# Three of eight tiles with seven products in the second feed-forward matrix, one bank moved last, and a split end for the first feed-forward block

## The chip, the cores and the metric

One core of a Trainium2 chip runs the whole program: TensorE (PE; PEld is its weight load), VectorE (DVE), ScalarE (ACT), GpSimd (POOL) and SyncE (SP), which issues the weight transfers. The metric is the device time in microseconds of one execution. The median of three runs of the kernel before is 2309.98 us (2309.74 to 2311.31).

## The reference, cut to what matters

Two layers of attention and feed-forward on 256 tokens of width 2048, all in float32. The change lies in the two feed-forward blocks (hidden width 8192) and in what follows the first of them, the norm of the dilated attention:

```
def sq_relu_mlp(h, w1, w2):
    return jnp.square(jax.nn.relu(h @ w1)) @ w2
...
        g, w1, w2 = ffns[i]
        x = x + sq_relu_mlp(rms_norm(x, g), w1, w2)
    return rms_norm(x, final_norm)
```

## The kernel before

**Products.** Every float32 operand of a large matrix product is split into an upper and a lower part (`hi`, `lo`), and each product of 128x128 by 128x512 is made of three matmuls (`three`, L193: upper by upper, upper by lower, lower by upper), which add into one of eight PSUM banks.

**Tiles.** A feed-forward block runs over four groups `g` of 2048 hidden columns. Each group makes two products with the first matrix and two with the second (`cp` 0 and 1, 1024 output columns each). Such a product (`gemm_pair`) is eight steps, one for each 256 rows of the contraction; a step is called a tile here and has the number of its rows (`pair`, 0 to 7). A standard tile (kind `s`) makes eight products for the four output quadrants, 24 matmuls. A seven-product tile (kind `x`) is one level of the Strassen-Winograd scheme: sums of weight quadrants against sums of the left operand's, seven products, 21 matmuls. `FF_PAIRS = (3, 5)`: two of the eight tiles of each product have seven products. Their seven sums gather in banks called "1" to "7", and "2", "3", "4" and "S" are also the four quadrants of the standard tiles. After the last seven-product tile `begin` combines "1", "6", "7" and "5" into an SBUF tile `C`; after the last tile `end` adds "2", "4", "S" and "3" to it.

**Order of the work.** The program is written out by hand: the last loop goes over `steps`, and in step i each of four quarters emits its matmuls, then its tasks (transposes), the functions in `after`, and the preparation `prep(i + 2, n)` of the tile two steps later; at the end of a step come `evac`, the last quarter's preparation, the load of step i + 5, and `post`. Each engine works through its own instructions in this order. Preparing a standard tile is two casts on ACT (`wh`, L190) and two subtractions on DVE (`wl`, L191). Preparing a seven-product tile (`prep_x`) is on DVE three additions into `sums` (L136), a `wl` of 128x1024, the subtraction `ls` of 128x2048 (L133) after ACT's cast `hs` (L176), and a `wl` of 128x512.

**Hidden values.** After a product with the first matrix, ACT squares the positive part of `C`, TensorE transposes it in the second and third tile of the next product (L694), into the four banks in `ps.spare` (the coming product's "1", "6", "7" and "5", in this order), and `post` of `hidden` splits the result into `hT`. For a seven-product tile of the second matrix `post` copies the transposed pair out (`h`) and makes its sums on DVE (`sums_and_parts`: `c`, `h`, `hT`, `hs`); for the others DVE makes one subtraction `hT` from the bank.

**After the second matrix** `residual` adds `C` to x in two additions of 128x1024 (x<-x,C). In the last group the squares for the next norm and the transposes of x follow (`next_norm`, `next_done`). In the second block, the last product's two last tiles are done column half by column half (`split_end`), so that half of x is complete one tile early.

Of the kernel before, what the change touches and what calls it, by code (L numbers as in the profile page):

```python
# [47 lines left out]
def tile_encoder(ctx: ExitStack, tc: tile.TileContext, ins, out):  # L48
# [217 lines left out]
    def sum_banks():  # L266

        if ps.order is None:
            l = ps.pair
            a, b = (l + 1) % 3, (l + 2) % 3  # L270
            ps.order = [2 * a, 2 * a + 1, 2 * b, 2 * b + 1, 6, 7, 2 * l, 2 * l + 1]
        order, ps.order = ps.order, ps.order[4:] + ps.order[:4]
        ps.spare = order[4:]
        return {q: order[n] for n, q in enumerate(("2", "4", "S", "3", "1", "6", "7", "5"))}

    STD = {(0, 0): "2", (0, 1): "3", (1, 0): "4", (1, 1): "S"}

    def gemm_pair(w, cp, A, sums_of, order, finish, split_end=False):
# [13 lines left out]
        def product(bank, a, b, last):  # L292
            if not q:
# [4 lines left out]
        X = (("1", "A11", 2), ("2", "A12", 3), ("6", "S2", 6), ("7", "S3", 4), ("5", "S1", 5), ("4", "A22", 7),  # L298
             ("3", "S4", 1))

        for n, (kind, pair) in enumerate(order):
# [7 lines left out]
            else:  # L309
                def quarter(s, m, pair=pair, n=n):  # L310
                    tb, c = ((0, 0), (1, 0), (1, 1), (0, 1))[m]
# [33 lines left out]

        def end(m):
            C = q["C"]
            if m == 0:
                add(nc.vector, C[:, 0, :], C[:, 0, :], q["2"])
            elif m == 1:  # L350
                subtract(nc.vector, C[:, 2, :], q["4"], C[:, 2, :])
            elif m == 2:
                add(nc.vector, C[:, 3, :], C[:, 3, :], q["S"])
            else:
                add(nc.vector, C[:, 1, :], C[:, 1, :], q["3"])
# [306 lines left out]

    FF_PAIRS = (3, 5)
    FF_ORDER = [("x" if k in FF_PAIRS else "s", k) for k in range(8)]
    FF_LAST = [FF_ORDER[k] for k in (0, 1, 3, 2, 5, 4, 6, 7)]

# [5 lines left out]
    def ffn(norm, w1, w2, next_norm, next_done):  # L672
        for g in range(4):
            hT, sums = [None] * 4, {}

            def hidden(made, q, cp, hT=hT, sums=sums):
# [7 lines left out]
                for m, (tb, n) in enumerate(((0, 0), (1, 0), (1, 1), (0, 1))):  # L684
                    at_after(i, m, lambda tb=tb, n=n: squared_relu(tb, n))
                for r in range(4):
# [10 lines left out]
                    def post(r=r, held=held):  # L697
# [3 lines left out]
                        if pair in FF_PAIRS:  # L701
                            raw = scratch([P, 2, T], "h")
                            nc.scalar.copy(raw, held["t"])
                            sums[pair] = part.pool.tile([P, 2, 3, P], F32R, name="hs", tag="hsum", bufs=len(FF_PAIRS))
# [7 lines left out]
            for cp in range(2):  # L712
                gemm_pair(w1, 2 * g + cp, norm.xT, norm.sums, FF_ORDER, lambda made, q, cp=cp: hidden(made, q, cp))

            w2g = w2[4 * g:4 * (g + 1)]
            last = g == 3

            def residual(made, q, cp):
                if last and next_norm() in fin and cp == 1:
                    def early():  # L720
                        add(nc.vector, x[:, 0, D // 2:], x[:, 0, D // 2:], both(q, 0))
                        subtract(nc.vector, x[:, 1, D // 2:D - 512], x[:, 1, D // 2:D - 512], q["C"][:, 2, :])
                        add(nc.vector, x[:, 1, D - 512:], x[:, 1, D - 512:], q["C"][:, 3, :])
                    made[-3].evac.append(early)
                    for tb in range(2):
                        made[-2].evac.append(lambda tb=tb: add(
# [387 lines left out]
```

## Time and profile before

| | |
|---|---|
| median of 3 runs | 2309.98 us (2309.74 to 2311.31) |
| the profiled execution's own time | 2308.4 us |
| its span, first to last instruction | 2306.6 us |
| busy: PE, PEld, DVE, ACT, POOL | 2273.0, 1898.0, 1758.8, 1217.7, 0.7 us |
| mean granted TensorE clock | 0.998 |

The span lies 1.8 us below the execution's own time, and that time 1.6 us below the median of the runs. A row of a timeline gives the start, the time taken, the engine, the line, the operation with output and inputs, and in brackets the idle time before it with the instruction that ended it. Matmuls and VectorE instructions overlap their successors a little: the distance between two starts is what one costs in a full queue.

### The profile page before, as it was taken

To read this page: it belongs to the slowest core of one execution; us is meant where nothing else is said; L and a number is where in the kernel's file an instruction comes from. 1 tells how busy PE (TensorE), PEld (TensorE's weight loads), DVE (VectorE), ACT (ScalarE), POOL (GpSimd) and SP (SyncE) were. 2 spreads that over 40 slices of the span, in tenths; PEclk is the share of its full clock that TensorE was granted. 3 is DMA by queue.
4 is the path that set the end of the run, shared out by engine and by line. 5 is a ranking of instruction groups with operands and counts; after the bars stand their busy time and mean duration, and the time that the engine had idled before them with its cause. 6 is when DMAs were issued, how large, how long until landed. Compare 5 with 4: busy or idle time off the path is not lost.

```text
span 2306.6 us, 28352 instructions
## 1 busy us (share of the span) xinstructions
PE 2273.0 (99%) x10988; PEld 1898.0 (82%) x10988; DVE 1758.8 (76%) x2082; ACT 1217.7 (53%) x1526; POOL 0.7 (0%) x6
## 2 busy tenths in 40 slices
PE   9999999999999999999999999999999999999998
PEld 7888888888888888887788888888888888888886
DVE  6666766788788788788877667757888788788787
ACT  6444545564564564565444544456554654554554
POOL 0000000000000000000000000000000000000000
PEclk9999999999999999999999999999999999999999
DMA  7555655656656656655554555555666566566563
GB/s 250 173 175 174 193 185 167 191 181 210 186 182 206 194 177 208 200 167 180 178 198 167 184 171 181 175 172 161 184 209 187 183 205 196 182 201 201 182 219 128
DMA packets 110727, 430.33 MB, mean 187 GB/s; under 512 B 23872, under 2 KB 24448, under 8 KB 92160
## 3 DMA queue, kind: packets, MB, share of 16 engines
q1 hardware_dynamic: 109920, 426.82, 57.4%
q8 instruction: 86, 1.41, 0.2%
q10 hardware_dynamic: 672, 1.70, 0.2%
q14 instruction: 49, 0.40, 0.0%
HBM read 426.38 MB, written 2.10 MB: 186 GB/s over the span
## 4 chain that ended last, share of the span: by engine, by line
PE 87%; DVE 5%; ACT 5%; issue 2%; DMA 1%; SPq 0%; ACTq 0%; DVEq 0%
PE banks L195 22%; PE banks L196 22%; PE banks L197 22%; PE banks L220 13%; PE banks L222 6%; ACT wh L190 2%; DVE wl L191 1%; DVE sums L136 1%; DVE ls L133 1%; ACT C L681 1%; ACT hs L176 1%; PE banks L694 1%; PE banks L384 1%; ACT C L682 0%; DMA bias<-in_rpb_dram 0%
## 5 line engine op out<-in xcount | busy, mean ns | idle before, releaser
L191 DVE TENSOR_TENSOR wl<-w,wh 128x1024 fp32r<-128x1024 f32 (+1 forms) x802 | 931.5, 1176 | 389.5 <-ACT wh L190 385.7
L190 ACT CAST wh<-w 128x1024 fp32r<-128x1024 f32 (+1 forms) x802 | 804.6, 1014 | 691.6 <-PE banks L197 478.4
L220 PE MATMUL banks<-xT,wh 128*128 128x512 f32 x1280 | 455.6, 399 | 0.5 <-ACT wh L190 0.4
L195 PE MATMUL banks<-wh,xT 128*128 128x512 f32 x1152 | 453.7, 394 | 0.0
L197 PE MATMUL banks<-wh,xT 128*128 128x512 f32 x1152 | 449.3, 390 | 0.0
L196 PE MATMUL banks<-wl,xT 128*128 128x512 f32 x1152 | 448.6, 389 | 0.6 <-DVE wl L191 0.6
L222 PE MATMUL banks<-xT,wl 128*128 128x256 f32 x1280 | 358.5, 280 | 2.3 <-DVE wl L191 2.3
L195 PE MATMUL banks<-wh,hT 128*128 128x512 f32 x832 | 327.2, 393 | 0.0
L197 PE MATMUL banks<-wh,hT 128*128 128x512 f32 x832 | 324.4, 390 | 0.0
L196 PE MATMUL banks<-wl,hT 128*128 128x512 f32 x832 | 323.8, 389 | 0.0
L220 PEld LDWEIGHTS banks<-xT,wh 128*128 128x128 f32 x1280 | 241.6, 189 | 55.6 <-ACT wh L190 1.5
L197 PEld LDWEIGHTS banks<-wh,xT 128*128 128x128 f32 x1152 | 216.2, 188 | 45.8
L196 PEld LDWEIGHTS banks<-wl,xT 128*128 128x128 f32 x1152 | 216.5, 188 | 43.9 <-DVE wl L191 0.9
L195 PEld LDWEIGHTS banks<-wh,xT 128*128 128x128 f32 x1152 | 216.5, 188 | 42.7
L222 PEld LDWEIGHTS banks<-xT,wl 128*128 128x128 f32 x1280 | 242.4, 189 | 3.7 <-DVE wl L191 3.4
L176 ACT CAST hs<-sums 128x2048 fp32r<-128x2048 f32 x64 | 122.5, 1914 | 156.5 <-DVE sums L136 156.5
L197 PEld LDWEIGHTS banks<-wh,hT 128*128 128x128 f32 x832 | 156.2, 188 | 33.0
L196 PEld LDWEIGHTS banks<-wl,hT 128*128 128x128 f32 x832 | 156.4, 188 | 31.8
L195 PEld LDWEIGHTS banks<-wh,hT 128*128 128x128 f32 x832 | 156.3, 188 | 31.3
L133 DVE TENSOR_TENSOR ls<-sums,hs 128x2048 fp32r<-128x2048 f32 x64 | 146.7, 2292 | 43.6 <-ACT hs L176 43.6
L136 DVE TENSOR_TENSOR sums<-sums,w 128x512 f32<-128x512 f32 x128 | 88.6, 692 | 4.4
L136 DVE TENSOR_TENSOR C<-C,banks 128x512 f32<-128x512 f32 x125 | 82.5, 681 | 0.0
(190 smaller groups left out, 2137.7 us busy)
## 6 DMA issues: line engine op xcount, KB each, us to landing
w<-in_ffn_w_dram SPq DMA_DIRECT2D x512, 512.0 KB, 5.0
w<-in_dil_wqkv_dram SPq DMA_DIRECT2D x72, 1024.0 KB, 4.9
w<-in_na_wqkv_dram SPq DMA_DIRECT2D x47, 1024.0 KB, 5.2
w<-in_na_wo_dram SPq DMA_DIRECT2D x16, 1024.0 KB, 4.9
w<-in_dil_wo_dram SPq DMA_DIRECT2D x8, 1024.0 KB, 4.8
bias<-in_rpb_dram SPq DMA_DIRECT2D x32, 96.0 KB, 8.6
out_dram<-x SPq DMA_DIRECT2D x8, 256.0 KB, 2.5
x<-in_x_dram SPq DMA_DIRECT2D x3, 512.0 KB, 9.0
```

Source lines behind the costliest of these rows:

```text
L133: engine.tensor_tensor(out=out, in0=a, in1=b, op=ALU.subtract)
L136: engine.tensor_tensor(out=out, in0=a, in1=b, op=ALU.add)
L176: nc.scalar.copy(s.hs, s.sums)
L190: nc.scalar.copy(dst_hi, src)
L191: nc.vector.tensor_tensor(out=dst_lo, in0=src, in1=dst_hi.bitcast(F32), op=ALU.subtract)
L195: nc.tensor.matmul(o, left[0], right[0], start=start, stop=False)
L196: nc.tensor.matmul(o, left[0], right[1], start=False, stop=False)
L197: nc.tensor.matmul(o, left[1], right[0], start=False, stop=stop)
L220: nc.tensor.matmul(o, s.hi[a][:, cs], xt.rearrange("p h t -> p (h t)"), start=first, stop=False)
L222: nc.tensor.matmul(o[:, :T], s.lo[a][:, cs], xt[:, 0, :], start=False, stop=last)
L384: nc.tensor.transpose(self.tp[:, a, tb * P:(tb + 1) * P], x[:, tb, kt * P:(kt + 1) * P], ident)
L681: nc.scalar.activation(c, c, AF.Relu, scale=norm.r[:, tb:tb + 1])
```

## The change

1. In groups 0 to 2 of both blocks the second matrix has three seven-product tiles (3, 5, 6); their order is 0 1 2 3 4 5 6 7 in the first column block (`cp` 0) and 0 1 3 2 5 6 4 7 in the second. Group 3 keeps 3 and 5.
2. In a seven-product tile bank "5" comes last; it came fifth of seven.
3. `begin` has three parts, and combines the seven-product sums alone in `C`. For the first matrix `last_sum` adds the four quadrants' banks to `C`. For the second matrix the banks are added to x directly (`put`, x<-x,banks) and the rows of `C` apart from that (`early`), by a DMA that adds or by DVE.
4. The first block's last product gets `split_end` too, with its norm's squares and transposes half by half, and the tile order 0 1 2 4 3 5 6 7.

```
-        X = (("1", "A11", 2), ("2", "A12", 3), ("6", "S2", 6), ("7", "S3", 4), ("5", "S1", 5), ("4", "A22", 7),
-             ("3", "S4", 1))
+        X = (("1", "A11", 2), ("2", "A12", 3), ("6", "S2", 6), ("7", "S3", 4), ("4", "A22", 7), ("3", "S4", 1),
+             ("5", "S1", 5))
...
             if m == 0:
                 C = q["C"] = part.pool.tile([P, 4, 512], F32, name="C", tag="C")
                 nc.scalar.copy(C[:, 0, :], q["1"])
-                q["U"] = scratch([P, 512], "U")
-                subtract(nc.vector, q["U"], q["6"], C[:, 0, :])
+                subtract(nc.vector, C[:, 1, :], q["6"], C[:, 0, :])
             elif m == 1:
-                subtract(nc.vector, q["C"][:, 2, :], q["U"], q["7"])
+                subtract(nc.vector, q["C"][:, 2, :], q["7"], q["C"][:, 1, :])
             elif m == 2:
-                add(nc.vector, q["C"][:, 1, :], q["U"], q["5"])
-            else:
-                add(nc.vector, q["C"][:, 3, :], q["C"][:, 2, :], q["5"])
...
+                add(nc.vector, q["C"][:, 1, :], q["C"][:, 1, :], q["5"])
+                subtract(nc.vector, q["C"][:, 3, :], q["5"], q["C"][:, 2, :])
...
-        for m in range(4):
-            s.after[m].append(lambda m=m: begin(m))
-            if not split_end:
-                made[-1].after[m].append(lambda m=m: end(m))
+        for m in range(3):
+            s.after[0 if s is made[-1] else m].append(lambda m=m: begin(m))
...
+    def last_sum(q, tb, c, out):
+
+        add(nc.vector, out, q["C"][:, 2 * tb + c, :], q[STD[tb, c]])
...
         for g in range(4):
+            last = g == 3
+            pairs2 = FF_PAIRS if last else (3, 5, 6)
...
-            def residual(made, q, cp):
...
-                def rows(tb):
-                    to = x[:, tb, cp * 1024:(cp + 1) * 1024]
-                    add(nc.vector, to, to, both(q, tb))
-                made[-1].evac.append(lambda: rows(1))
-                made[-1].evac.append(lambda: rows(0))
...
+            def residual(made, q, cp, parted):
+                def put(tb, c):
+                    add(nc.vector, to(cp, tb, c), to(cp, tb, c), q[STD[tb, c]])
+
+                def early(n):
+                    o = x[:, n, cp * 1024:(cp + 1) * 1024]
+                    rows = q["C"][:, 2 * n:2 * n + 2, :].rearrange("p a n -> p (a n)")
+                    if last:
+                        add(nc.vector, o, o, rows)
+                    else:
+                        nc.gpsimd.dma_start(o, rows, accum_op=ALU.add)
+
+                if not parted:
+                    for m, (tb, c) in enumerate(QUARTERS):
+                        made[-1].after[m].append(lambda tb=tb, c=c: put(tb, c))
+                    for n in range(2):
+                        (made[-1].after[n] if last else made[-1].evac).append(lambda n=n: early(n))
...
+                for n in range(2):
+                    made[-2 if next_done is not None else -3].evac.append(lambda n=n: early(n))
+                for tb in range(2):
+                    made[-2].after[1 + 2 * tb].append(lambda tb=tb: put(tb, 0))
+                made[-2].post.append(lambda: next_norm().squares(NB - 2))
...
+                for tb in range(2):
+                    made[-1].after[1 + 2 * tb].append(lambda tb=tb: put(tb, 1))
+                made[-1].post.append(lambda: next_norm().squares(NB - 1))
+                made[-2].post.append(lambda: ps.spare.extend([ps.taken["2"], ps.taken["4"]]))
+                next_done(made[-2], NB - 2)
+                next_done(made[-1], NB - 1)
...
+                parted = last and cp == 1
+                order = range(8)
+                if parted:
+                    order = ((0, 1, 2, 4, 3, 5, 6, 7), (0, 1, 3, 2, 5, 4, 6, 7))[next_done is None]
+                elif cp and not last:
+                    order = 0, 1, 3, 2, 5, 6, 4, 7
```

`early` runs when its step is written out, in the last loop. By then `ffn` has returned, and its name `last`, which `early` reads at that moment, has the value of the last group. So the branch with the DMA is not taken in any group: in the built program GpSimd's list is the same eleven rows as before, with no DMA, and the rows of `C` are added on VectorE.

In the built program the order of VectorE's instructions moves at three places. The first is the third tile of the second matrix's first column block in groups 0 to 2, where the transposed hidden values of tiles 5, 6 and 7 are split. Before (`c`, `h` and `hs` are tile 5's sums, the two `hT` from banks are tiles 6 and 7, the `wl` between them are tile 4's weights):

```order
L133 TENSOR_TENSOR hT<-h,hT 128x2x256
L133 TENSOR_TENSOR hs<-c,hs 128x384
L191 TENSOR_TENSOR wl<-w,wh 128x512
L191 TENSOR_TENSOR hT<-banks,hT 128x2x256
L191 TENSOR_TENSOR wl<-w,wh 128x1024
L191 TENSOR_TENSOR hT<-banks,hT 128x2x256
L191 TENSOR_TENSOR wl<-w,wh 128x1024
```

The same place on VectorE in the changed kernel:

```order
L133 TENSOR_TENSOR hs<-c,hs 128x384
L191 TENSOR_TENSOR wl<-w,wh 128x512
L133 TENSOR_TENSOR c<-h 128x128
L133 TENSOR_TENSOR h<-h 128x128
L133 TENSOR_TENSOR c<-h 128x128
L133 TENSOR_TENSOR c<-h,c 128x128
L133 TENSOR_TENSOR hT<-h,hT 128x2x256
L133 TENSOR_TENSOR hs<-c,hs 128x384
L191 TENSOR_TENSOR wl<-w,wh 128x1024
L191 TENSOR_TENSOR hT<-banks,hT 128x2x256
```

Six instructions stand where tile 6 had one, ahead of tile 7's `hT`, which frees the fourth spare bank, "5".

The second place is the rest of that product on VectorE: the preparation of tiles 5, 6, 7 and of the next product's first two, and the sums into `C` and x. Before, from tile 5's `ls`:

```order
L133 TENSOR_TENSOR ls<-sums,hs 128x2048
L191 TENSOR_TENSOR wl<-w,wh 128x512
L191 TENSOR_TENSOR wl<-w,wh 128x1024 x4
L133 TENSOR_TENSOR U<-banks,C 128x512
L133 TENSOR_TENSOR C<-U,banks 128x512
L191 TENSOR_TENSOR wl<-w,wh 128x1024
L136 TENSOR_TENSOR C<-U,banks 128x512
```

In the changed kernel, from tile 6's preparation, which follows tile 5's without a row between:

```order
L136 TENSOR_TENSOR sums<-w 128x1024
L136 TENSOR_TENSOR sums<-sums,w 128x512 x2
L191 TENSOR_TENSOR wl<-w,wh 128x1024
L133 TENSOR_TENSOR ls<-sums,hs 128x2048
L191 TENSOR_TENSOR wl<-w,wh 128x512
L191 TENSOR_TENSOR wl<-w,wh 128x1024 x4
L133 TENSOR_TENSOR C<-banks,C 128x512 x2
L136 TENSOR_TENSOR C<-C,banks 128x512
L133 TENSOR_TENSOR C<-banks,C 128x512
L136 TENSOR_TENSOR x<-x,banks 128x512 x2
L191 TENSOR_TENSOR wl<-w,wh 128x1024
L136 TENSOR_TENSOR x<-x,banks 128x512 x2
```

After these rows stand `x<-x,C 128x1024 x2`, as before. The four sums into x take the place of the four last sums into `C`; the number of sums is the same, and tile 6's preparation has four rows more than two `wl`.

The third place is the end of the first feed-forward block on VectorE, its last two tiles (the `wl` are the first attention step's). Before:

```order
L136 TENSOR_TENSOR C<-C,banks 128x512
L133 TENSOR_TENSOR C<-banks,C 128x512
L191 TENSOR_TENSOR wl<-w,wh 128x1024
L136 TENSOR_TENSOR C<-C,banks 128x512 x2
L136 TENSOR_TENSOR x<-x,C 128x1024 x2
L191 TENSOR_TENSOR wl<-w,wh 128x1024
```

After:

```order
L191 TENSOR_TENSOR wl<-w,wh 128x1024
L136 TENSOR_TENSOR C<-C,banks 128x512
L133 TENSOR_TENSOR C<-banks,C 128x512
L136 TENSOR_TENSOR x<-x,banks 128x512
L136 TENSOR_TENSOR x<-x,C 128x1024 x2
L191 TENSOR_TENSOR wl<-w,wh 128x1024
L136 TENSOR_TENSOR x<-x,banks 128x512
L191 TENSOR_TENSOR wl<-w,wh 128x1024
L401 TENSOR_SCALAR gx<-banks,gT 128x256
L403 TENSOR_TENSOR xT<-gx,xT 128x256
```

The additions of `C` to x move one tile earlier, the third column block's `gx` and `xT` follow inside the last tile, and the last x<-x,banks of the fourth column block stands behind four such pairs.

More of the change, by code (lines that the diff above doesn't have):

```diff
@@ L273, in sum_banks @@
         ps.spare = order[4:]
-        return {q: order[n] for n, q in enumerate(("2", "4", "S", "3", "1", "6", "7", "5"))}
+        ps.taken = {q: order[n] for n, q in enumerate(("2", "4", "S", "3", "1", "6", "7", "5"))}
+        return ps.taken
+    QUARTERS = (0, 0), (1, 0), (1, 1), (0, 1)
     STD = {(0, 0): "2", (0, 1): "3", (1, 0): "4", (1, 1): "S"}
@@ L661, in begin_norm, with ff_order @@
         return pending_norm(lambda: norms[n], n == 2)
+    def ff_order(pairs, order=range(8)):
+        return [("x" if k in pairs else "s", k) for k in order]
     FF_PAIRS = (3, 5)
-    FF_ORDER = [("x" if k in FF_PAIRS else "s", k) for k in range(8)]
-    FF_LAST = [FF_ORDER[k] for k in (0, 1, 3, 2, 5, 4, 6, 7)]
     parts = {len(steps) + 9: "feed-forward"}
@@ L712, in ffn @@
             for cp in range(2):
-                gemm_pair(w1, 2 * g + cp, norm.xT, norm.sums, FF_ORDER, lambda made, q, cp=cp: hidden(made, q, cp))
+                gemm_pair(w1, 2 * g + cp, norm.xT, norm.sums, ff_order(FF_PAIRS), lambda made, q, cp=cp: hidden(made, q, cp))
             w2g = w2[4 * g:4 * (g + 1)]
-            last = g == 3
-            def residual(made, q, cp):
[L719 to L724, printed above, removed]
-                    for tb in range(2):
-                        made[-2].evac.append(lambda tb=tb: add(
-                            nc.vector, x[:, tb, D // 2:D - 512], x[:, tb, D // 2:D - 512], q[STD[tb, 0]]))
-                    made[-2].post.append(lambda: fin[0].squares(NB - 2))
-                    made[-1].after[1].append(lambda: fin[0].finish(0, q["3"]))
-                    made[-1].after[3].append(lambda: fin[0].finish(1, q["S"]))
-                    return
-                def rows(tb):
-                    to = x[:, tb, cp * 1024:(cp + 1) * 1024]
-                    add(nc.vector, to, to, both(q, tb))
-                made[-1].evac.append(lambda: rows(1))
-                made[-1].evac.append(lambda: rows(0))
-                if last:
-                    for c in (2 * cp, 2 * cp + 1):
-                        made[-1].post.append(lambda c=c: next_norm().squares(c))
-                        if next_done is not None:
-                            next_done(made[-1], c, c % 2)
@@ L744, in both, with to @@
-            def both(q, tb):
-                return q["C"][:, 2 * tb:2 * tb + 2, :].rearrange("p a n -> p (a n)")
-            for cp in range(2):
-                end = last and next_norm() in fin and cp == 1
-                gemm_pair(w2g, cp, hT, sums, FF_LAST if end else FF_ORDER,
-                          lambda made, q, cp=cp: residual(made, q, cp), split_end=end)
+            def to(cp, tb, c):
+                return x[:, tb, cp * 1024 + c * 512:cp * 1024 + (c + 1) * 512]
+            def residual(made, q, cp, parted):
[13 more added lines that the diff above has]
+                        (made[-1].after[n] if last else made[-1].evac).append(lambda n=n: early(n))
+                    if last:
+                        for c in (2 * cp, 2 * cp + 1):
+                            made[-1].post.append(lambda c=c: next_norm().squares(c))
+                            if next_done is not None:
+                                next_done(made[-1], c, c % 2)
+                    return
+                for n in range(2):
[3 more added lines that the diff above has]
+                made[-2].post.append(lambda: next_norm().squares(NB - 2))
+                if next_norm() in fin:
+                    for tb in range(2):
+                        made[-1].after[1 + 2 * tb].append(lambda tb=tb: fin[0].finish(tb, lambda: put(tb, 1)))
+                    return
+                for tb in range(2):
[4 more added lines that the diff above has]
+                next_done(made[-1], NB - 1)
@@ L1045, in tile_encoder @@
         run_late()
[L1046 to L1047 removed]
+        if i:
+            p = steps[i - 1]
+            p.w = p.hi = p.lo = p.hs = p.sums = None
     part.end()
```

30 lines of the change are left out of this document (10 added, 20 removed).

## The prediction

> **What bounds the kernel now.** I read the page first. TensorE is busy for 99% of the span, VectorE for 76%.
>
> ```profile
> span 2306.6 us, 28352 instructions
> PE 2273.0 (99%) x10988; PEld 1898.0 (82%) x10988; DVE 1758.8 (76%) x2082; ACT 1217.7 (53%) x1526; POOL 0.7 (0%) x6
> ```
>
> So a matmul less is time less, unless the work that feeds it takes longer than the matmuls it saves; and since 76% is a mean over stages, the place of the change decides. The waits of TensorE came second (time in total, times, longest):
>
> ```profile
> PE banks L195 <- DVE hT L191: 6.9, 8, 0.9
> PE banks L196 <- DVE ls L133: 3.3, 3, 1.4
> ...
> ```
>
> The eight waits for `hT` come once per group, in both blocks, at the same place: tile 3 of the second matrix's first product, where bank "5" is first written. That is the timeline I read third, group 1 of the first block. TensorE (start, time taken, idle before):
>
> ```profile
> 685.44 0.39 PE L195 MATMUL banks<-wh,hT 128*128 128x512 f32 x1
> ...
> 687.96 0.40 PE L197 MATMUL banks<-hs 128*128 128x512 f32 x1
> 689.22 0.50 PE L195 MATMUL banks<-hs,hT 128*128 128x512 f32 x1 [0.87 <-DVE hT L191]
> ...
> 691.42 0.39 PE L195 MATMUL banks<-wh,hT 128*128 128x512 f32 x1
> ...
> 696.87 0.39 PE L195 MATMUL banks<-wh,hT 128*128 128x512 f32 x1
> ...
> 698.24 0.39 PE L195 MATMUL banks<-hs 128*128 128x512 f32 x1
> ...
> 701.73 0.39 PE L195 MATMUL banks<-wh,hT 128*128 128x512 f32 x1
> ...
> 754.99 0.39 PE L195 MATMUL banks<-wh,xT 128*128 128x512 f32 x1
> ```
>
> Tile 3, with seven products, begins at 685.44 and tile 4 at 691.42, tile 5 at 696.87, tile 6 at 701.73; the second product of this group ends where the next group's first matrix begins, at 754.99. A standard tile thus takes 696.87 - 691.42 = 5.45 us, a seven-product tile 701.73 - 696.87 = 4.86: a replaced tile saves 0.59, less than three times a matmul's 0.23, for its matmuls stand a little farther apart. At 689.22 bank "5" comes late: the matmul before began at 687.96 and is followed after 0.23 where nothing waits, so the wait costs 689.22 - 688.19 = 1.03.
>
> VectorE at the same place:
>
> ```profile
> 683.54 0.28 DVE L133 TENSOR_TENSOR c<-h 128x128 f32<-128x128 f32 x1
> ...
> 685.97 0.69 DVE L191 TENSOR_TENSOR wl<-w,wh 128x512 fp32r<-128x512 f32 x1
> 686.57 0.69 DVE L191 TENSOR_TENSOR hT<-banks,hT 128x512 fp32r<-128x512 f32 x1
> 687.34 1.23 DVE L191 TENSOR_TENSOR wl<-w,wh 128x1024 fp32r<-128x1024 f32 x1
> 688.48 0.68 DVE L191 TENSOR_TENSOR hT<-banks,hT 128x512 fp32r<-128x512 f32 x1
> ...
> 690.22 1.22 DVE L136 TENSOR_TENSOR sums<-w 128x1024 f32<-128x1024 f32 x1
> ...
> 694.87 2.29 DVE L133 TENSOR_TENSOR ls<-sums,hs 128x2048 fp32r<-128x2048 f32 x1 [0.84 <-ACT hs L176]
> 697.07 4.09 DVE L191 TENSOR_TENSOR wl<-w,wh 128x512 fp32r<-128x512 f32 x4
> 703.01 1.23 DVE L191 TENSOR_TENSOR wl<-w,wh 128x1024 fp32r<-128x1024 f32 x1 [1.85 <-ACT wh L190]
> ...
> 712.33 1.28 DVE L136 TENSOR_TENSOR C<-C,banks 128x512 f32<-128x512 f32 x2
> 713.52 2.35 DVE L136 TENSOR_TENSOR x<-x,C 128x1024 f32<-128x1024 f32 x2
> 715.80 2.35 DVE L191 TENSOR_TENSOR wl<-w,wh 128x1024 fp32r<-128x1024 f32 x2
> ```
>
> Rows left out are marked; from tile 5's sums of hidden values (683.54) until tile 6's preparation there is hardly a pause. Tile 7's `hT`, which empties bank "5", begins at 688.48, and 689.22 is when TensorE may write it. The first pauses are 0.84 (VectorE waits for ScalarE's cast `hs`, at every seven-product tile) and 1.85 at 703.01. VectorE is thus already the late engine here, with little in reserve, and it is this engine that the change loads.
>
> **What one thing costs on VectorE**, from distances between starts. A seven-product tile's preparation: from 690.22 to 697.07 is 6.85 to the end of `ls`, and its last `wl` of 128x512 takes 686.57 - 685.97 = 0.60, together 7.45, the pause of 0.84 in it. A standard tile's: two `wl` of 688.48 - 687.34 = 1.14, so 2.28. A sum from a bank: (713.52 - 712.33)/2 = 0.60. The two additions of `C` to x: 715.80 - 713.52 = 2.28. The hidden sums of a seven-product tile: 685.97 - 683.54 = 2.43; of a standard one 0.60.
>
> **The change, part by part.** *DMAs that add.* In the built program there are none, for `early` reads `last` when the loop has ended: the additions of 2.28 stay on VectorE in all products, GpSimd has nothing to do, and no transfer is added.
>
> *Three seven-product tiles in groups 0 to 2.* TensorE saves 0.59 in two products of six groups, 7.1 us in all. VectorE gains in each product 7.45 - 2.28 = 5.17, and once per group 2.43 - 0.60 = 1.83 for tile 6's hidden sums. Adding up its queue for one group, from where it was at 690.22: tile 6's sums come ahead of tile 7's `hT`, 1.83, and I add 0.2 (an estimate: ScalarE casts tile 6's values twice, so tile 4's weights come a little later), so tile 5's sums begin at 692.25. Bank "5" is free 2.03 later than before, at 691.25; being last of the seven it is wanted six matmuls later, at 688.19 + 6 x 0.23 = 689.57: a wait of 1.7 in place of 1.03. From 692.25 VectorE has, up to the end of `ls` of the second product's tile 6: four whole preparations of seven-product tiles (5 and 6 of the first product, 3 and 5 of the second), 29.8; the fifth, tile 6, until its `ls`, 6.85; four standard tiles (7, 0, 1, 2), 9.1; four sums in `begin` and four into x, 4.8; the additions of `C`, 2.28. Sum 52.8: the last `ls` is done at 745.1. Nothing in that list waits for TensorE, since each buffer is free before VectorE comes to it: the longest reach is the upper half of a `wl` two tiles ahead, and by this sum TensorE is always past there.
>
> TensorE from 685.44, without waits: five seven-product tiles (3, 5, 6; 3, 5) 24.3, five standard ones 27.25, and 698.24 - 696.87 = 1.37 plus one matmul, 0.23, until tile 6 of the second product needs its `ls`: 53.15, that is 738.6. So TensorE must wait 6.5 us in all (about 1.7 at bank "5", 2.7 at tile 6 of the first product, 2.0 at tile 6 of the second). From 745.1 there remain 4.86 - 1.6 = 3.26 and two standard tiles, 10.9, and 0.1 of restart: the group ends at 759.4 to 759.5 where it ended at 754.99, **+4.5 us**. Six such groups: **+27.0**. The next group begins as before, since its first tiles are standard and VectorE catches up there.
>
> The bounds of this: the pause of 0.84 in five preparations is the one doubtful item; if ScalarE hid it, 4.2 less, and a group costs 0.3, six 2. It stood in the queue at 694.87 when VectorE was late, so I keep it. The upper bound is below, with the clock.
>
> *Bank "5" last, in group 3 of both blocks:* wanted at 689.57 in the terms above, free at 689.22; the wait of 1.03 goes, twice: **-2.1**. In the first matrix nothing waits, so nothing is gained.
>
> *`begin` in three parts, sums to x from the banks:* as many instructions of the same size, in the last tile, where VectorE had pauses; no cost of its own in group 3. In groups 0 to 2 they are in the sum above.
>
> *Split end of the first block.* TensorE's waits there, and one at the end of the second block:
>
> ```profile
> 1065.00 0.66 PE L384 MATMUL banks<-ident,x 128*128 128x128 f32 x4 [0.43 <-DVE x L136]
> 1083.65 0.50 PE L196 MATMUL banks<-ls,hs 128*128 128x512 f32 x1 [1.37 <-DVE ls L133]
> 1095.10 0.50 PE L196 MATMUL banks<-ls,hs 128*128 128x512 f32 x1 [0.75 <-DVE ls L133]
> 1112.67 0.66 PE L384 MATMUL banks<-ident,x 128*128 128x128 f32 x4 [0.34 <-DVE x L136]
> 1119.60 0.66 PE L384 MATMUL banks<-ident,x 128*128 128x128 f32 x4 [0.19 <-DVE gx L410]
> 1121.31 0.71 PE L427 MATMUL banks<-ident,rw 128*128 128x128 f32 x4 [1.05 <-DVE gx L410]
> 1125.29 0.65 PE L384 MATMUL banks<-ident,x 128*128 128x128 f32 x4 [1.86 <-DVE gx L410]
> 2266.14 0.50 PE L196 MATMUL banks<-ls,hs 128*128 128x512 f32 x1 [1.16 <-DVE ls L133]
> ```
>
> The first three, 2.55, are VectorE's lateness after the first product of group 3. There the additions of `C` to x move into the last tile's quarters, where VectorE waited for the banks, so the norm starts 2.28 earlier, and tile 3 comes one tile later: I count 2.55 gained. The last four before 1126, 3.44, come from the transposes of x. What takes their place must be counted on VectorE and ScalarE:
>
> ```profile
> 1109.55 1.05 ACT L190 CAST wh<-w 128x1024 fp32r<-128x1024 f32 x1 [1.66 <-PE banks L197]
> 1118.21 0.48 DVE L410 TENSOR_SCALAR gx<-banks,gT 128x256 f32<-128x256 f32 x1
> ...
> 1121.63 2.35 DVE L191 TENSOR_TENSOR wl<-w,wh 128x1024 fp32r<-128x1024 f32 x2
> ```
>
> In the last tile but one, from its third quarter's end (4.1 us in), stand a cast (1.05) with its `wl` (1.14), two sums (1.2), a sum into x (0.6) and the additions of `C` (2.28): 10.4. TensorE wants the third column block of x after half of the last tile, at 5.45 + 2.7 = 8.2: a new wait of 2.2. The fourth block's last sum stands behind two `wl`, a sum and four pairs of `gx` and `xT` (1121.63 - 1118.21 = 3.4), and ScalarE's casts and squares between: at some 18.5, where TensorE wants it at 16.8, 1.7. So 3.9 for 3.44; together **-2.1**. Bounds: -6 if none of the new waits comes, +3 if they are twice as long.
>
> *The second block's end:* 1.16 at 2266.14 stays about as it is, since TensorE arrives 1.03 earlier and the additions of `C` are done up to 2.28 earlier: 0, between -1.2 and +1.
>
> **Sum.** 27.0 - 2.1 - 2.1 = +22.8 us against the profiled execution's 2308.4, which is 1.6 below the median of 2309.98: on the median's scale 2332.8, so **2333 us**, slower by 1.0%.
>
> **The clock.** A wait may cost more than itself. Three stretches (length, busy time of PE, PEld, DVE, ACT, POOL, granted clock, DMA share, GB/s):
>
> ```profile
> 1083.60:1087.00 3.40, 3.35 (x14) 2.59 (x15) 3.33 (x7) 0.04 (x1) 0.00 (x0) 1.00 0.12 10
> ...
> 1122.00:1126.00 4.00, 2.14 (x14) 1.66 (x13) 3.93 (x7) 0.02 (x1) 0.00 (x0) 1.00 0.53 158
> 1126.00:1130.00 4.00, 4.00 (x15) 3.41 (x14) 2.76 (x6) 1.86 (x3) 0.00 (x0) 0.57 0.26 109
> ```
>
> After the wait of 1.86 at 1125.29 the granted clock was 0.57 for 4 us, a loss of 0.43 x 4 = 1.7; after the 1.37 at 1083.65 it stayed at 1.00. The new waits, 1.7, 2.7 and 2.0, lie around that. After the first two of them the loss would only shorten the next wait, since VectorE sets when that ends; after the third it is added, 1.7 per group, 10 in all. I take none in the sum and all of it for the range's upper end. [...]
>
> **Rivals.**
> *VectorE hides it (faster).* TensorE saves 7.1, the eight waits of 1.03 go, 8.2, and the split end 2.1: 2310 - 17.4 = 2293. For it: VectorE is idle for a quarter of the span, and paused 1.85 at 703.01. Against it: it decides where the queue has 6.5 us less between 690 and 745, and the pauses of that stretch in before are what the extra 12.2 us (two preparations and tile 6's sums) fill. Chance 0.05.
> *The DMAs do run,* or VectorE is shorter by as much for another reason: 2.28 less ahead of the last `ls`, 13.7 in six groups: 2319. Against it: GpSimd's list. Chance 0.08.
> *The clock falls after the third wait:* up to 2343. Chance 0.14.
> *All cancels,* within 0.2%, 4.6 us, about what can be told from no change here: 0.03.
> *My forecast,* 2326 to 2338: 0.70.
>
> Slower by over 0.2% then has 0.92, the same 0.03, faster 0.05. The range, 2321 to 2343, leaves out the first and fourth rival and most of the second.
>
> **What would show it.** In the changed trace: TensorE's waits for `ls` grow from 3.3 to some 28 us and come twice per group in groups 0 to 2; the wait for `hT` stays in six groups at about 1.5 and is gone from group 3; VectorE is busy some 63 us more (12 x 4.33 and 6 x 1.83; 1759 to 1822) and without a pause but the 0.84 through these stretches; GpSimd and the DMA queues are as before; the matmuls are 36 fewer. I am wrong if VectorE pauses there for anything but `hs`, or if TensorE's waits for `ls` stay below 10 us.

## The result and the profile after

| | before | after |
|---|---|---|
| median | 2310.22 us (2309.74 to 2311.31, 4 runs) | 2334.94 us (2334.43 to 2335.30, 4 runs) |
| ratio, 95% interval | | 1.0106 [1.0089, 1.0124] |
| the profiled execution, its span | 2308.4, 2306.6 us | 2335.3, 2333.5 us |

The change makes the kernel 1.1% slower; 2333 was forecast. The line of busy times of the changed kernel's page, and the line of its chain that gives the shares of the engines:

```profile
PE 2274.6 (97%) x10952; PEld 1889.3 (81%) x10952; DVE 1818.1 (78%) x2159; ACT 1235.5 (53%) x1550; POOL 0.7 (0%) x6
...
PE 72%; DVE 14%; ACT 7%; issue 5%; DMA 2%; SPq 0%; ACTq 0%; DVEq 0%
```

TensorE has 36 matmuls fewer and is idle for longer; VectorE has 59 us more work. VectorE's and ScalarE's shares of the chain were 5% each and are 14% and 7%. TensorE's waits (total, times, longest):

```profile
PE banks L196 <- DVE ls L133: 22.2, 20, 1.5
PE banks L195 <- DVE hT L191: 9.1, 6, 1.5
...
PE banks L196 <- DVE wl L191: 4.5, 8, 0.6
```

The same group as in the prediction, group 1 of the first block. TensorE's timeline; the first row begins the second matrix, the last the next group:

```profile
675.18 0.39 PE L195 MATMUL banks<-wh,hT 128*128 128x512 f32 x1
...
699.20 0.50 PE L195 MATMUL banks<-hs,hT 128*128 128x512 f32 x1 [1.52 <-DVE hT L191]
...
711.52 0.50 PE L196 MATMUL banks<-wl,hT 128*128 128x512 f32 x1 [0.56 <-DVE wl L191]
...
714.65 0.51 PE L196 MATMUL banks<-ls,hs 128*128 128x512 f32 x1 [1.47 <-DVE ls L133]
...
736.49 0.50 PE L196 MATMUL banks<-ls,hs 128*128 128x512 f32 x1 [0.42 <-DVE ls L133]
...
753.69 0.50 PE L196 MATMUL banks<-ls,hs 128*128 128x512 f32 x1 [1.47 <-DVE ls L133]
...
767.93 0.39 PE L195 MATMUL banks<-wh,xT 128*128 128x512 f32 x1
```

The second matrix takes 767.93 - 675.18 = 92.75 us. The row of before that begins it is

```profile
667.25 0.39 PE L195 MATMUL banks<-wh,hT 128*128 128x512 f32 x1
```

so it took 754.99 - 667.25 = 87.74 there: 5.01 more, in spite of 1.2 us fewer matmuls. VectorE in the changed kernel, with every pause of more than 0.1 us between 698 and 753 shown:

```profile
700.20 1.22 DVE L136 TENSOR_TENSOR sums<-w 128x1024 f32<-128x1024 f32 x1
...
704.85 2.29 DVE L133 TENSOR_TENSOR ls<-sums,hs 128x2048 fp32r<-128x2048 f32 x1 [0.85 <-ACT hs L176]
...
712.30 2.29 DVE L133 TENSOR_TENSOR ls<-sums,hs 128x2048 fp32r<-128x2048 f32 x1 [0.84 <-ACT hs L176]
...
734.15 2.29 DVE L133 TENSOR_TENSOR ls<-sums,hs 128x2048 fp32r<-128x2048 f32 x1 [0.85 <-ACT hs L176]
...
743.88 2.29 DVE L133 TENSOR_TENSOR ls<-sums,hs 128x2048 fp32r<-128x2048 f32 x1 [0.84 <-ACT hs L176]
...
751.34 2.29 DVE L133 TENSOR_TENSOR ls<-sums,hs 128x2048 fp32r<-128x2048 f32 x1 [0.84 <-ACT hs L176]
753.55 5.31 DVE L191 TENSOR_TENSOR wl<-w,wh 128x512 fp32r<-128x512 f32 x5
```

The five pauses are the five seven-product preparations of the stretch, each waiting for ScalarE's `hs`, which ScalarE begins when VectorE has made the `sums` and for which it takes 1.91. They are 4.2 us of the list; whether another order of the preparation would close them was not run. Apart from them VectorE does nothing else than work through its list, and TensorE's last wait ends at 753.69, with the last `ls`.

Where the span's 26.9 us come from, by starts of the stages: the six products with the second matrix in groups 0 to 2, 6 x 5.01 = 30.1; the second matrix in the last group of the first block +0.3 and the dilated attention behind it -4.9 (both together the last group's bank "5", the split end, and some 1.7 of the lowered clock in before, granted at 0.50 for 3.41 us); the end of the second block -1.3; the attention ahead of the first block +3.0, whose code is the same; the other stages together -0.1 (the terms are rounded). The first attention took 404.93 us in the profile of before and between 405.6 and 407.9 in all profiles since, so the 3.0 say nothing of the change.

### The profile page after: what moved, and what is told of

Same layout as the page of the kernel before. It is cut to its first block, busy times and chain, and to the rows that moved or that the text cites. A ratio compares the mean times of both kernels' runs of the same rounds, so it can differ in the third digit from the quotient of the medians.

```text
span 2333.5 us, 28381 instructions
## 1 busy us (share of the span) xinstructions
PE 2274.6 (97%) x10952; PEld 1889.3 (81%) x10952; DVE 1818.1 (78%) x2159; ACT 1235.5 (53%) x1550; POOL 0.7 (0%) x6
## 3 DMA queue, kind: packets, MB, share of 16 engines
q8 instruction: 85, 1.39, 0.2%
## 4 chain that ended last, share of the span: by engine, by line
PE 72%; DVE 14%; ACT 7%; issue 5%; DMA 2%; SPq 0%; ACTq 0%; DVEq 0%
PE banks L196 17%; PE banks L197 17%; PE banks L195 17%; PE banks L220 13%; PE banks L222 6%; DVE sums L136 4%; DVE wl L191 4%; ACT hs L176 3%; DVE ls L133 2%; ACT wh L190 2%; DVE x L136 1%; DMA bias<-in_rpb_dram 1%; PE banks L689 1%; ACT C L675 1%; PE banks L375 1%
## 5 line engine op out<-in xcount | busy, mean ns | idle before, releaser
L190 ACT CAST wh<-w 128x1024 fp32r<-128x1024 f32 (+1 forms) x802 | 793.2, 1006 | 617.2 <-PE banks L197 405.7
L196 PE MATMUL banks<-wl,hT 128*128 128x512 f32 x760 | 297.2, 391 | 3.4 <-DVE wl L191 3.4
L195 PE MATMUL banks<-wh,hT 128*128 128x512 f32 x760 | 299.9, 395 | 0.0
L197 PE MATMUL banks<-wh,hT 128*128 128x512 f32 x760 | 296.8, 391 | 0.0
L176 ACT CAST hs<-sums 128x2048 fp32r<-128x2048 f32 x76 | 145.4, 1913 | 233.8 <-DVE sums L136 233.8
L133 DVE TENSOR_TENSOR ls<-sums,hs 128x2048 fp32r<-128x2048 f32 x76 | 174.2, 2293 | 54.5 <-ACT hs L176 54.5
L196 PEld LDWEIGHTS banks<-wl,hT 128*128 128x128 f32 x760 | 142.9, 188 | 36.9 <-DVE wl L191 8.4
L197 PEld LDWEIGHTS banks<-wh,hT 128*128 128x128 f32 x760 | 142.7, 188 | 30.0
L195 PEld LDWEIGHTS banks<-wh,hT 128*128 128x128 f32 x760 | 142.8, 188 | 28.6
L136 DVE TENSOR_TENSOR sums<-sums,w 128x512 f32<-128x512 f32 x152 | 105.2, 692 | 5.2
L136 DVE TENSOR_TENSOR sums<-w 128x1024 f32<-128x1024 f32 x76 | 92.6, 1218 | 0.0
```

What stands on the lines that cost most here:

```text
L133: engine.tensor_tensor(out=out, in0=a, in1=b, op=ALU.subtract)
L136: engine.tensor_tensor(out=out, in0=a, in1=b, op=ALU.add)
L176: nc.scalar.copy(s.hs, s.sums)
L190: nc.scalar.copy(dst_hi, src)
L195: nc.tensor.matmul(o, left[0], right[0], start=start, stop=False)
L196: nc.tensor.matmul(o, left[0], right[1], start=False, stop=False)
```

## The experiments

The theory: the time of a group is set by the length of VectorE's list ahead of the second product's last `ls`, so each instruction taken off that list, or put behind it, shortens each of the six groups by its own length until TensorE's own time is reached. Rivals: the third tile costs nothing by itself and the time is lost elsewhere; another engine can do VectorE's additions for less; the waits are single buffers that come late and can be mended by moving one tile. The measure in each is the distance from the second matrix's first matmul in group 1 of the first block to the next group's first.

| kernel | median, us | ratio to before, 95% | second matrix, group 1 |
|---|---|---|---|
| before | 2310.22 | | 87.74 |
| after | 2334.94 | 1.0106 [1.0089, 1.0124] | 92.75 |
| two tiles | 2296.71 | 0.9946 [0.9931, 0.9961] | 86.60 |
| DMA adds | 2321.20 | 1.0052 [1.0036, 1.0069] | 90.41 |
| sums on GpSimd | 2414.20 | 1.0452 [1.0436, 1.0468] | 104.10 |
| bank last alone | 2299.00 | 0.9957 [0.9942, 0.9971] | 86.60 |
| 5 and 6 apart | 2323.48 | 1.0057 [1.0043, 1.0071] | 90.73 |
| first matrix | 2300.72 | 0.9961 [0.9948, 0.9973] | 86.59 |
| second product only | 2292.47 | 0.9925 [0.9911, 0.9939] | 86.02 |
| tile 1 as third | 2309.62 | 0.9996 [0.9982, 1.0010] | 88.76 |

Each ratio is to runs of the kernel before beside the experiment; their medians were 2310.35 (two tiles, DMA adds, sums on GpSimd, bank last), 2310.08 (5 and 6 apart, first matrix, second product) and 2309.69 (tile 1 as third).

**Two tiles again, the rest of the change kept.**

```diff
-            pairs2 = FF_PAIRS if last else (3, 5, 6)
+            pairs2 = FF_PAIRS
...
-                elif cp and not last:
-                    order = 0, 1, 3, 2, 5, 6, 4, 7
```

> The changed kernel with tiles 3 and 5 alone as seven-product tiles in all groups (order 0 to 7); bank '5' last, the sums into x and the split end stay. Theory (VectorE's queue in the second matrix of groups 0 to 2 sets the time): the second matrix of these groups takes 87.7 - 1.0 = 86.7 us in place of 92.8, six times -6.1, so about 2298 us, and no wait of TensorE for ls in groups 0 to 2. Rival (the other parts of the change, the sums into x or the bank's place, cost the time): 2310 or more, with waits left in groups 0 to 2.

2296.71 us. TensorE's waits for `ls` as they stand now, and the start and end of the second matrix in group 1:

```profile
PE banks L196 <- DVE ls L133: 2.1, 2, 1.2
```

```profile
667.37 0.39 PE L195 MATMUL banks<-wh,hT 128*128 128x512 f32 x1
...
753.97 0.39 PE L195 MATMUL banks<-wh,xT 128*128 128x512 f32 x1
```

The twenty waits for `ls` become two, both at the ends of the blocks, and the wait for `hT` has no row any more. 86.60 us is the group without a wait, for standard tiles and two seven-product tiles. So the third tile costs 38.2 us by the medians (36.9 by the groups, 6 x 6.15), and the rest of the change gains 13.6 (2310.35 - 2296.71). This is the fastest kernel here that computes all of the reference, 0.5% below the kernel before.

**Bank "5" last alone,** in the kernel before.

```diff
-        X = (("1", "A11", 2), ("2", "A12", 3), ("6", "S2", 6), ("7", "S3", 4), ("5", "S1", 5), ("4", "A22", 7),
-             ("3", "S4", 1))
+        X = (("1", "A11", 2), ("2", "A12", 3), ("6", "S2", 6), ("7", "S3", 4), ("4", "A22", 7), ("3", "S4", 1),
+             ("5", "S1", 5))
```

> The kernel before with one edit, bank '5' last of the seven. Theory: it is wanted 1.37 us later and the wait was 1.03, so all eight waits for hT go: 2310 - 8.2 = 2302 us. Rival (the time turns up at the next late row, tile 5's ls, which has 0.3 us to spare then): 2306 to 2310 us with new waits for ls.

2299.00 us: 11 of the 13.6 us. The waits for `hT` are all gone, and those for `ls` are as in the kernel before:

```profile
PE banks L196 <- DVE ls L133: 3.1, 3, 1.4
```

Each of the eight groups gains 87.74 - 86.60 = 1.14, so a wait of 0.87 in the brackets costs 1.14: the bracket is counted from the modelled end of the matmul before (0.39 after its start, where the next would start after 0.23), and the first matmul after the wait takes 0.50 instead of 0.39. Eight of them are 9.1; of the remaining 2.2 the clock accounts for 1.5 in the two profiles, which the last section shows.

The kernel with two tiles differs from this one by the split end and the parts of `begin`: 2.3 us less by the medians. By the stages, the second matrix in the first block's last group is 3.0 longer there and the stretch behind it 4.2 shorter; 1.7 of the 3.0 is the clock, granted at 0.50 for 3.41 us from 1104.87 in that profile.

**The DMAs that add, made to run.**

```diff
-                def early(n):
+                def early(n, last=last):
```

> The changed kernel with the value of last bound when early is defined, so that in groups 0 to 2 the rows of C are added to x by 24 DMAs of 512 KB from GpSimd. Theory (VectorE's queue): 2.28 us less in the queue ahead of the last ls of each of six groups, the second product's additions do not count: 2335 - 13.7 = 2321 us, with waits for ls still there and the first product's unchanged. Rival 1 (transfers collide with the weights' loads): 2335 or more and waits for weights. Rival 2 (the additions were the cause of it all): 2310 or less.

2321.20 us, 13.7 below the changed kernel, 2.3 per group. The waits and the transfers:

```profile
PE banks L196 <- DVE ls L133: 11.5, 9, 1.5
PE banks L195 <- DVE hT L191: 9.1, 6, 1.5
```

```profile
w<-in_ffn_w_dram SPq DMA_DIRECT2D x512, 512.0 KB, 5.2
...
x<-C POOLq DMA_DIRECT2D x24, 512.0 KB, 9.4
```

2.28 us off VectorE's list make this group 92.75 - 90.41 = 2.34 shorter: the list's length passes to the time one for one. The waits of the first product, for `hT`, `wl` and `ls`, which stand ahead of these additions, do not change. They are why the kernel stays slower than before, with 3.8 us per group over the 86.60; at the last `ls` TensorE is now held up by less than 0.2 us, so that a still shorter list behind the first product would bring hardly more. The 24 transfers take 9.4 us each, in the median, to land. The weights land after 5.2 instead of 5.1, and once VectorE waits for them, 0.44 us, in the first group of the first block, whose second matrix takes 90.95.

**The additions for `sums` on GpSimd.**

```diff
-            add(nc.vector, t[:, 0:2, :], w[:, 1:3, :], w[:, 0, :].unsqueeze(1).to_broadcast([P, 2, 512]))
+            add(nc.gpsimd, t[:, 0:2, :], w[:, 1:3, :], w[:, 0, :].unsqueeze(1).to_broadcast([P, 2, 512]))
```

and likewise the two additions after it.

> The changed kernel with the three additions of weights into sums on GpSimd in place of VectorE, in every seven-product tile. Theory (VectorE's queue): 2.58 us less per seven-product tile, 12.9 less ahead of the last ls, more than TensorE's whole wait there; if GpSimd takes no more than about 5 us for the three, the second matrix of groups 0 to 2 falls to about 85.5 us and the run to some 2290 us. Rival 1 (GpSimd is slow, or slows VectorE): TensorE waits for sums, hs or ls as before or longer, 2320 to 2400 us. Rival 2 (ScalarE's cast hs and not VectorE is the late one): ls still late by about as much, 2330 us.

2414.20 us: the kernel becomes slower by another 79. GpSimd's groups (count, busy, mean ns of one, idle), and three of VectorE's:

```profile
L136 POOL TENSOR_TENSOR sums<-sums,w 128x512 f32<-128x512 f32 x152 | 276.5, 1819 | 11.9
L136 POOL TENSOR_TENSOR sums<-w 128x1024 f32<-128x1024 f32 x76 | 201.5, 2652 | 1881.6 <-DMA w<-in_ffn_w_dram 1647.7 <-DVE ls L133 117.5 <-DVE wl L191 50.2
```

```profile
L191 DVE TENSOR_TENSOR wl<-w,wh 128x1024 fp32r<-128x1024 f32 x722 | 993.9, 1394 | 352.4 <-ACT wh L190 349.6
...
L136 DVE TENSOR_TENSOR x<-x,C 128x1024 f32<-128x1024 f32 x32 | 51.8, 1653 | 0.6
L136 DVE TENSOR_TENSOR x<-x,banks 128x512 f32<-128x512 f32 x64 | 41.3, 680 | 0.9 <-PE banks L197 0.9
```

The same rows of the changed kernel:

```profile
L191 DVE TENSOR_TENSOR wl<-w,wh 128x1024 fp32r<-128x1024 f32 x722 | 873.1, 1221 | 343.1 <-ACT wh L190 339.9
...
L136 DVE TENSOR_TENSOR x<-x,banks 128x512 f32<-128x512 f32 x64 | 41.4, 680 | 0.9 <-PE banks L197 0.9
L136 DVE TENSOR_TENSOR x<-x,C 128x1024 f32<-128x1024 f32 x32 | 37.9, 1221 | 0.6
```

Three things go wrong. GpSimd needs 2.65 + 2 x 1.82 = 6.3 us for what took 2.6 on VectorE, so `hs` and `ls` come later (TensorE now waits 21 us for `hs`). Several of VectorE's instructions take longer in this run (means): x<-x,C 1.65 instead of 1.22, the `wl` of 128x1024 1.39 instead of 1.22, the c<-h of 128x128 0.673 instead of 0.289, and of the norms a copy 0.538 instead of 0.295 and two scalar instructions 0.66 instead of 0.170, four of each. Others do not: `ls` stays at 2.29 and x<-x,banks, with one input in a bank, at 0.680. What decides which of them become longer, no run here shows. Third, the clock: fourteen times ahead of the kernel's end it was granted at 0.50 for 3.41 or 6.83 us, 75 us in all, while in the changed kernel this did not happen once; the means of the two profiles are 0.983 and 0.999. TensorE was busy for 63 of these 75 us, so at most half of that, 31 of the 79 us, is the clock's (an estimate). The run thus does not tell what a faster engine for these additions would be worth.

**Tiles 5 and 6 apart** in the second product.

```diff
-                    order = 0, 1, 3, 2, 5, 6, 4, 7
+                    order = 0, 1, 3, 2, 5, 4, 6, 7
```

> The changed kernel with the second product's tiles of the second matrix in the order 0 1 3 2 5 4 6 7 in groups 0 to 2, so that a standard tile stands between its last two seven-product tiles; the work is the same. Theory (what counts is how much VectorE has queued ahead of the last ls against what TensorE has ahead of it): tile 6 comes one standard tile later, 5.45 us for TensorE and 2.28 for VectorE, so the waits in the second product (0.4 and 1.5) go and those in the first stay: about 2 us less in each of six groups, 2322 us. Rival (the amount of VectorE's work in the group counts, wherever it stands): 2333 to 2336 us.

2323.48 us, and the group in TensorE's timeline

```profile
672.13 0.39 PE L195 MATMUL banks<-wh,hT 128*128 128x512 f32 x1
...
762.86 0.39 PE L195 MATMUL banks<-wh,xT 128*128 128x512 f32 x1
```

is 90.73 us, 2.0 less. With tile 4 ahead of tile 6, TensorE gets a standard tile (5.45 us) more before the last `ls`, and VectorE 2.3 us of `wl` more; the difference, 3.2, is more than the last wait was worth. The waits ahead of it, for `hT` and at tile 6 of the first product, are as they were. The order of the tiles was thus a part of the loss, 2.0 of the 6.15 us per group.

**The third tile in the second product alone** (tile 1, in the kernel with two tiles; the second product of the first matrix in the order 0 1 2 4 3 6 5 7).

```diff
-            pairs2 = FF_PAIRS
+            pairs2 = FF_PAIRS if last else (1, 3, 5)
...
+                elif cp and not last:
+                    order = 0, 2, 3, 4, 5, 6, 1, 7
-                gemm_pair(w2g, cp, hT, sums, ff_order(pairs2, order), ...
+                gemm_pair(w2g, cp, hT, sums, ff_order(pairs2 if cp else FF_PAIRS, order), ...
```

In this kernel and in the one on the first matrix below, one product of a group takes the third tile as a standard one with the left operand's quadrant A21 - A22 in A21's place, so that part of the sum is another number; the instructions are those of a standard tile.

> The run with two seven-product tiles, and a third one (tile 1, whose hidden sums are made one product earlier) in the second product of the second matrix alone, groups 0 to 2, order 0 2 3 4 5 6 1 7; the first matrix's second product in the order 0 1 2 4 3 6 5 7 there. Theory: bank '5' is free in time, since tile 6 keeps its one instruction, and the three tiles have standard ones between them: 0.59 saved six times, 3.5 less than 2296.7, about 2293 us. Rival (three tiles in this product overload VectorE whatever their order, since the additions into x stand in it): 2297 to 2306 us with waits for ls in the second product.

2292.47 us. TensorE's timeline in group 1:

```profile
666.65 0.39 PE L195 MATMUL banks<-wh,hT 128*128 128x512 f32 x1
...
752.67 0.39 PE L195 MATMUL banks<-wh,xT 128*128 128x512 f32 x1
```

86.02, against 86.60: 0.58 gained of the 0.59 that a replaced tile saves, and no new wait for `ls`. The first matrix gains 0.25 in these groups as well (86.83 to 86.56), by its new order, which the 2293 did not count. One extra preparation per group, placed late, fits into VectorE's pauses; this is where the idle quarter of VectorE's time is real.

**Tile 1 as the third in both products** (the first matrix in the same order as in the run above).

```diff
-            pairs2 = FF_PAIRS
+            pairs2 = FF_PAIRS if last else (1, 3, 5)
...
+                elif not last:
+                    order = ((0, 2, 4, 3, 6, 5, 1, 7), (0, 2, 3, 4, 5, 6, 1, 7))[cp]
```

> The run with two seven-product tiles, and tile 1 as the third one in both products of the second matrix, groups 0 to 2 (orders 0 2 4 3 6 5 1 7 and 0 2 3 4 5 6 1 7), with the first matrix's second product in the order 0 1 2 4 3 6 5 7 there: as many matmuls as the changed kernel, another place. Theory (VectorE's queue against TensorE's): tile 1's hidden sums are made in the first matrix, where VectorE has room, so bank '5' is free in time; the second product saves 0.59 per group; in the first product the last ls is wanted 2.7 - 2.05 = 0.65 us too early, which takes up its 0.59. So 3.5 us less than 2296.7, and up to 1.6 more from the first matrix's new order, 2291.5 to 2293.5 us. Rival (three seven-product tiles in both products are too much wherever the third stands): above 2300 us with waits for ls in both products.

2309.62 us, no different from the kernel before, and 16 above what I expected; the rival came true. TensorE's waits for `ls` in group 1 (there is one more, 0.33 for `hT`):

```profile
705.76 0.50 PE L196 MATMUL banks<-ls,hs 128*128 128x512 f32 x1 [1.47 <-DVE ls L133]
...
727.65 0.50 PE L196 MATMUL banks<-ls,hs 128*128 128x512 f32 x1 [0.38 <-DVE ls L133]
```

I had taken each wait by itself: bank "5" nearly on time, so its 1.7 gone, and the 2.7 at the first product's third seven-product tile less the 2.03 by which the hidden sums leave the list (the prediction's 1.83 + 0.2). But a TensorE that does not wait at bank "5" is at the next wait 1.7 us earlier, and finds the same VectorE. By the list, worked out after the run, it comes out: 92.75 - 2.03 - 2.0 (the tiles apart, as above) = 88.7; measured 88.76. The two effects add, and 2.1 us per group of excess remain over 86.6.

**The third tile in the first matrix,** where VectorE has more room.

```diff
-    out_rows(ins["na_wo"], na_oT, 4, lambda: norms[1], begin_norm(1, False, FF_PAIRS),
+    out_rows(ins["na_wo"], na_oT, 4, lambda: norms[1], begin_norm(1, False, (3, 5, 6)),
...
+                gemm_pair(w1, 2 * g + cp, norm.xT, norm.sums,
+                          ff_order(FF_PAIRS) if cp else ff_order((3, 5, 6), (0, 1, 3, 2, 5, 4, 6, 7)), ...
```

> The run with two seven-product tiles, and a third one (6) in the first of the two products with the first matrix in all eight groups, order 0 1 3 2 5 4 6 7, a standard tile between any two of seven products; the norm makes the sums for tile 6 once per block. Theory (a third tile pays where VectorE has room): no hidden values are split during that product, a seven-product and a standard tile are 7.45 + 2.28 = 9.7 us of VectorE against 10.3 of TensorE, so TensorE saves 0.59 eight times: 4.7 less than 2296.7, about 2292 us, 24 matmuls fewer and no new waits for ls. Rival (VectorE is full everywhere, a third tile never pays): 2297 us or more, with waits for ls in these products.

2300.72 us, 4 slower than with two tiles, where 5 faster was expected. In groups 1 to 3 the first matrix gains what was expected (86.80 to 86.21 each). In group 0 of the two blocks it loses 2.2 and 3.7, and there TensorE's timeline has a wait that I had not counted; this is the first block's:

```profile
422.31 0.50 PE L195 MATMUL banks<-hs,xs 128*128 128x512 f32 x1 [2.50 <-DVE xT L406]
```

In group 0 a bank of the first seven-product tile still holds the norm's transposes; the new order puts tile 3 third instead of fourth, one tile earlier, and the bank is wanted before VectorE has emptied it. It is the same kind of wait as at bank "5". The second block has it too, 2.51 long, and there the clock fell behind it, to 0.50 from 1605.44 to 1608.85, which is the 1.5 more (last section). So the miss is explained by the order in group 0; a version with the old order there was not run.

## Why the prediction was right

*The sign and its cause.* VectorE's list decides in groups 0 to 2: shown by its rows without a pause but the 0.84, by the run with two tiles, whose group has no wait left, and by the edit that takes 2.28 off the list and 2.34 off the group. Two edits that only move work along the list take off 2.0 and 4.0; the first was forecast, the second was accounted for after its run.

*The queue sum.* Tile 5's sums were forecast for 692.25; the changed kernel's second matrix starts 7.93 later than in before (675.18 - 667.25), so for 700.18, and they start at 700.20. The last `ls` was to be done at 745.1 + 7.93 = 753.0; the next instruction starts at 753.55. The 52.8 us of the list were 53.35, and with that a group costs 5.01 instead of 4.5, six of them 30.1 instead of 27.0. This is the largest mis-sized term. Some 0.3 of the 0.55 lies in the four sums of `begin` in the first product, which took 722.44 - 719.72 = 2.72 where 2.4 was counted.

*The waits.* 20 for `ls` with 22.2 us and 8 for `wl` with 4.5, against some 28 for `ls`. There are three for `ls` in each of the six groups (1.47, 0.42, 1.47), not two: part of what I put at tile 6 of the second product comes at tile 3 of it, and part of what I put at tile 6 of the first at a `wl`. When one list decides, its total can be forecast, but not well at which tile TensorE will stand. The six for `hT` are 1.5 each, as forecast, and there is none in group 3. VectorE's busy time rose to 1818, 1822 was forecast; GpSimd and the DMA queues are as before.

*Group 3 and the ends.* I took -1.03 for each bank "5", -2.1 for the split end and 0 for the second block's end, -4.2 in all. Measured: -4.6 for the first block's last product and what follows, -1.3 at the second's end, -5.9. Of the first block's -4.6 the bank is 1.1, and the split end with the parts of `begin` 2.0: from the start of the last group's second matrix to the second block's first matmul the changed kernel takes 1608.88 - 1034.23 = 574.65, and the run with bank "5" alone 1591.44 - 1014.80 = 576.64. TensorE's waits around the split end:

```profile
1109.83 0.50 PE L196 MATMUL banks<-ls,hs 128*128 128x512 f32 x1 [1.15 <-DVE ls L133]
...
1122.79 0.33 PE L375 MATMUL banks<-ident,x 128*128 128x128 f32 x1 [1.25 <-DVE x L136]
1123.93 0.55 PE L375 MATMUL banks<-ident,x 128*128 128x128 f32 x3 [0.81 <-DVE x L136]
1131.21 0.33 PE L375 MATMUL banks<-ident,x 128*128 128x128 f32 x1 [0.71 <-DVE gx L401]
1132.27 0.55 PE L375 MATMUL banks<-ident,x 128*128 128x128 f32 x3 [0.73 <-DVE x L136]
```

The new waits, forecast at 2.2 and 1.7, are 1.25 + 0.81 = 2.06 and 0.71 + 0.73 = 1.44. But not all of the 2.55 at the start went: one wait for `ls`, 1.15, stayed, since tile 5 still follows tile 3. What is left of the 4.6 is the clock of before, which behind its last wait there was at 0.50 for 3.41 us (1.7).

*The clock.* The rival that the third wait would lower it did not come. In these groups and at the split end TensorE's single waits were 1.5 us at most, and the granted clock stayed at full (length, busy times, granted clock, DMA share, GB/s):

```profile
751.00:755.00 4.00, 2.53 (x12) 1.73 (x11) 3.66 (x3) 3.67 (x5) 0.00 (x0) 1.00 0.11 44
1124.00:1128.00 4.00, 4.00 (x22) 3.39 (x23) 2.63 (x3) 2.73 (x7) 0.00 (x0) 1.00 0.45 145
```

At the split end the same two waits, 1.25 and 0.8, went either way. In the run with two tiles (1.25 and 0.80 at 1102.83 and 1103.96) and in the one with tile 1 as the third (1.25 and 0.81 at 1107.72 and 1108.85) the matmuls of 128x512 behind them start 0.43 us apart (from 1105.18 to 1105.61, from 1109.98 to 1110.41); here and in the run with the second product only (1.25 and 0.81 at 1100.66 and 1101.80) they start 0.23 apart. The waits that I forecast there thus did not tell whether the clock would fall.

*What lay in the forecast's favour.* The profile of before had the shortest first attention of all; its span compared with the changed kernel's gives 3 us that no edit made, and they happen to lie on the side of my low group term. By terms the change costs 30.1 - 5.9 = 24.2; I said 22.8; the medians say 24.7. That the total is off by no more is in part luck: the groups were taken 3.1 too low, and the ends gained 1.7 more than I took, most of it the clock of before, which no term of mine held.

## What to carry to other kernels

Where one engine feeds another from a list in fixed order, add up the whole list up to the last thing that is wanted, instead of pricing each wait: a wait that is removed comes back at the next place, until the list itself is shorter. Trade matmuls for preparation only where the feeding engine has pauses in that stretch: here a third seven-product tile was worth its 0.58 us in one of two products, and in both it cost 2 to 6 us per group, by its place. And take a change of several parts apart, for here the small parts were worth 13.6 us, hidden under the large one's 38.

## What the runs showed of the hardware

The clock after a short wait is not fixed. In before, the granted clock was 0.50 for 3.41 us after TensorE's wait of 1.86 (the 0.57 over 4 us of the prediction). With bank "5" moved, the same wait is there with the same length,

```profile
1122.68 0.66 PE L384 MATMUL banks<-ident,x 128*128 128x128 f32 x4 [1.86 <-DVE gx L410]
```

and the clock stayed at 1.00 (length, busy time of PE, PEld, DVE, ACT, POOL, granted clock, DMA share, GB/s):

```profile
1122.00:1126.00 4.00, 3.31 (x21) 2.95 (x21) 3.07 (x9) 1.89 (x3) 0.00 (x0) 1.00 0.56 233
1126.00:1130.00 4.00, 4.00 (x27) 3.56 (x26) 2.48 (x4) 1.05 (x1) 0.00 (x0) 1.00 0.47 125
```

The stretch behind the block was 1.5 us shorter (486.22 to 484.69).

The run with the third tile in the first matrix shows the same within one execution: its wait of 2.5 us comes twice. The first ends at 422.31, in the second of these rows, and the matmuls behind it start 0.23 us apart, as in a full queue; the second, 2.51 long, was followed by a granted clock of 0.50:

```profile
417.60:421.01 3.41, 2.21 (x10) 1.50 (x8) 3.34 (x5) 3.38 (x7) 0.00 (x0) 1.00 0.00 0
421.01:424.42 3.41, 2.11 (x9) 1.75 (x10) 3.41 (x6) 1.69 (x2) 0.00 (x0) 1.00 0.16 19
1602.02:1605.44 3.42, 0.91 (x5) 0.45 (x3) 3.42 (x5) 3.42 (x6) 0.00 (x0) 1.00 0.00 0
1605.44:1608.85 3.41, 3.41 (x8) 2.71 (x9) 3.41 (x4) 0.32 (x1) 0.00 (x0) 0.50 0.49 119
```

So in these traces the length of a wait did not tell whether the clock would fall: after 1.86 it fell in one and not in another, and after 2.5 once of twice. Where it fell in before and in the run with two tiles, it stayed at 0.50 for 3.41 us, and with TensorE busy throughout that is some 1.7 us of time (half of 3.41, an estimate). What decides whether it falls, the runs do not show.

Additions on GpSimd of 128x512 took 1.82 us where VectorE takes 0.69. In the run with these VectorE's `wl` of 128x1024 took 0.17 us longer in the mean and its x<-x,C of 128x1024 0.43, while `ls` of 128x2048 stayed at 2.29. A transfer of 512 KB that adds within SBUF took 9.4 us to land in the median, and the weights in the same run 5.2 instead of 5.1.
